# Two-layer diffusion backbone: the experts' down product moved behind the next pair's up products

## The chip, the cores and the metric

The kernel runs on one core of one Trainium2 chip. Its engines work side by side, each through its own instructions in order: TensorE (PE, matmuls; PEld is its weight load), VectorE (DVE), ScalarE (ACT), GpSimd (POOL) and SyncE (SP), which issues the DMAs. They wait for each other through semaphores. The metric is the device time of one execution in microseconds (us); lower is better.

## The reference

Two layers over 256 latent and 256 context tokens of width 1024, each a token mixer and then a mixture of experts; the mixers are not touched by the change. What is computed in the experts, for each of 32 of them, and what follows at the end:

```
pg = softmax(x @ wg + bg); grp = top1(pg)              # one of 4 groups
gate = pg_top * pe_top / sum(pe_top)                   # two of the 8 experts inside it
y_e = (silu(x_e @ w1[e]) * (x_e @ w3[e])) @ w2[e]      # w1, w3: 1024 x 512, w2: 512 x 1024
h_lat = h_lat + m_lat[:, 5] * sum over the token's experts of gate * y_e
h_ctx = h_ctx + m_ctx[5] * the same                    # layer 0 only
...
return rms_norm(h_lat, final_norm_g)                   # after layer 1
```

All weights are float32: 6.3 MB an expert, 201 MB a layer. Layer 0 works on 512 tokens (four tiles of 128), layer 1 on the 256 latent ones (two tiles).

## The kernel before

The experts of a layer are `moe(l, tiles, ...)`. It goes through them in 16 pairs; four experts (two pairs) share a group `eg`. Each expert has 64 slots for tokens (CAP).

- `prep(eg)` (DVE, L646) writes a mask `Pm` of ones for a group, 128 x 1024 in layer 0. It has one buffer, so it waits for the gathers that read the mask before it.
- `gather(eg, kk)` (PE, tile `ga`; L663, L664) multiplies the tokens by the mask, two of eight slices a call, and ACT copies the result to `xg` (L665). A pair does two of the four calls of the next group; the last group has no next one, so the last two pairs have no gathers.
- `up(p, q)` multiplies `xg` by w1 and w3 of expert q of pair p (tile `f`; L822, L824), then ACT applies silu and DVE multiplies (L826, L827), to `g`.
- `turn_hidden` transposes `g` (tile `gt`, L833), ACT copies it to `gT` (L835).
- `gated` (DVE, L673) and `spread` (tile `gg`, L680) make the scatter matrix `Gm` and the column of gates `gsl`.
- `down` multiplies `gT` by w2 (tile `y`, L846).
- `scaled` multiplies `y` by the gates and splits it into two float32r parts, `yh` by ACT (L855) and `yl` by DVE (L856).
- `scatter_items`: an item is one token tile and one half of the 1024 columns: two matmuls (tile `sc`; L692, L693), DVE multiplies by the modulation row `m5` into `tmp` (L695), POOL adds `tmp` to `h` (L696). Layer 0 has eight items a pair, layer 1 four. After the last pair's items ACT sums the squares of `h` (L699).

PE's order is written out by hand; the other engines' orders come from a scheduler. A pair's items are issued in the pair after it, in pieces: `some(nt // 2)` after the up products, a gather, `some(nt - 1)`, `turn_hidden`, `some(1)`, a gather, then the rest, `spread` and `down`. PSUM has four banks for `ga`, `gt`, `gg` and `sc` together (tag `x`), two for `f`, two for `y`; `tmp` has three buffers (NTMP).

Weights come in slots of 1 MB, twelve a pair: eight of w1 and w3, four of w2, in the order of `srcs`, through a ring of buffers (`wslot`, `fetch`, `take`); a slot is loaded again when the products that read it are done. After the last pair's down product stands `overflow`, a loop over experts with more than 64 tokens whose count is read at run time; all engines meet at it. The last pair's items run behind it. After layer 1 the program ends with the final norm: POOL multiplies `h[3]` by the norm's weight `fg` (L1653), DVE adds the two halves of the sums of squares (L1655), DVE and POOL make the reciprocal root (L312, L313), DVE and ACT scale the two tiles (L1657, L1658), SP stores them (L1660).

## Time and profile before

| | us |
|---|---|
| median of 3 runs (1604.54 to 1607.14) | 1605.23 |
| the profiled execution | 1606.87 |
| its span, first to last instruction | 1605.0 |
| PE busy in it | 1510.4 (94%) |
| DVE, ACT, POOL busy | 710.2, 490.5, 318.4 |

The experts of layer 0 lie between about 404 and 887 us of the span, those of layer 1 between about 1140 and 1597. Busy time of PE is the union of its matmuls, which overlap in their pipeline. In a timeline row the first number is the start, the second the duration of the row's instructions together, and the bracket names the idle time of the engine before them and what ended it.

### The profile page before, as it was taken

What the parts mean: (1) busy time and instruction counts of PE and PEld (TensorE: products, weight loads), DVE (VectorE), ACT (ScalarE), POOL (GpSimd) and SP (SyncE); (2) the same over time, 40 slices, a digit from 0 to 9 for tenths busy, and PEclk for the clock granted to TensorE, in tenths of its full rate; (3) what the DMA queues carried; (4) which work ended last, traced back from release to release, by engine and by line L of the source; (5) the groups of instructions that cost most, each with busy time, mean ns of one, the idle gap of its engine ahead of it and who ended that gap; (6) DMA issues with size and microseconds to landing.
All of it is one profiled execution on the core that took longest, in us unless ns stands there. A gap on an engine that the chain in (4) does not pass through costs nothing. (4 is left out here: it accounts for less than half of the span.)

```text
span 1605.0 us, 19381 instructions
## 1 busy us (share of the span) xinstructions
PE 1510.4 (94%) x7354; PEld 832.0 (52%) x7354; DVE 710.2 (44%) x1485; ACT 490.5 (31%) x913; POOL 318.4 (20%) x287
## 2 busy tenths in 40 slices
PE   6999999997999999999998899999899999999985
PEld 4676666676545455454443556777444443433432
DVE  2345685578135345344344566566323232322323
ACT  3326663372211111111111576665121111111111
POOL 1100021000025234243243311001012121211212
PEclk9999999998999999999999999999899999999997
DMA  9554435325999999999998665227899999999994
GB/s 322 200 210 159 156 109 184 105 105 212 374 380 420 420 420 419 420 419 420 420 420 338 247 237 178 86 93 275 323 407 419 421 419 421 420 420 420 420 421 164
DMA packets 96682, 498.35 MB, mean 310 GB/s; under 512 B 14132, under 2 KB 22628, under 8 KB 42180
## 3 DMA queue, kind: packets, MB, share of 16 engines
q1 hardware_dynamic: 96580, 497.02, 78.1%
q8 instruction: 61, 1.00, 0.3%
q14 instruction: 41, 0.34, 0.1%
HBM read 495.94 MB, written 1.05 MB: 310 GB/s over the span
## 5 line engine op out<-in xcount | busy, mean ns | idle before, releaser
L824 PE MATMUL f<-w,xg 128*64 128x512 f32 x1024 | 450.8, 594 | 16.4 <-DMA w<-in_w_dram 16.4
L822 PE MATMUL f<-w,xg 128*64 128x512 f32 x1024 | 450.7, 593 | 0.0
L824 PEld LDWEIGHTS f<-w,xg 128*64 128x64 f32 x1024 | 137.7, 137 | 203.3 <-issue 163.8
L695 DVE TENSOR_TENSOR tmp<-sc,m 128x512 f32<-128x512 f32 x192 | 128.2, 688 | 250.6 <-PE sc L693 242.0
L696 POOL TENSOR_TENSOR h_lat<-h_lat,tmp 128x512 f32<-128x512 f32 x124 | 157.7, 1286 | 394.9 <-DVE tmp L695 391.4
L846 PE MATMUL y<-w,gT 128*64 128x512 f32 x1024 | 226.8, 595 | 0.0
L822 PEld LDWEIGHTS f<-w,xg 128*64 128x64 f32 x1024 | 137.9, 137 | 118.1 <-issue 116.2
L826 ACT ACTIVATE g<-f 64x512 f32<-64x512 f32 x64 | 37.9, 593 | 410.7 <-PE f L824 276.5
L395 DVE TENSOR_TENSOR wlo<-w,whi 128x512 fp32r<-128x512 f32 x136 | 99.2, 735 | 124.1 <-ACT whi L394 118.2
L696 POOL TENSOR_TENSOR h_ctx<-h_ctx,tmp 128x512 f32<-128x512 f32 x62 | 85.2, 1387 | 333.8 <-DVE tmp L695 333.4
L846 PEld LDWEIGHTS y<-w,gT 128*64 128x64 f32 x1024 | 70.6, 137 | 133.4 <-issue 131.1
L394 ACT ACTIVATE whi<-w 128x512 fp32r<-128x512 f32 x136 | 88.7, 658 | 142.9 <-PE dacc L426 86.3
L425 PE MATMUL dacc<-x,whi 128*128 128x512 f32 (+1 forms) x320 | 127.4, 401 | 4.2 <-DVE rq L1354 2.7
L827 DVE TENSOR_TENSOR g<-g,f 64x512 f32<-64x512 f32 x64 | 43.9, 686 | 194.6 <-ACT g L826 193.7
L427 PE MATMUL dacc<-x,wlo 128*128 128x512 f32 (+1 forms) x320 | 119.9, 377 | 1.9 <-DVE wlo L395 1.8
L426 PE MATMUL dacc<-x,whi 128*128 128x512 f32 (+1 forms) x320 | 119.5, 374 | 0.0
L856 DVE SCALAR_TENSOR_TENSOR yhl<-y,gsl,yhl 128x1024 fp32r<-128x1024 f32 (+1 forms) x34 | 41.5, 1221 | 138.3 <-ACT yhl L855 136.8
L855 ACT ACTIVATE yhl<-y,gsl 128x1024 fp32r<-128x1024 f32 (+1 forms) x34 | 36.2, 1064 | 205.9 <-PE y L846 204.2
L692 PE MATMUL sc<-yhl,Gm 128*128 128x512 f32 x192 | 84.2, 439 | 10.5 <-issue 10.0
L663 PE MATMUL ga<-Pm,x 128*128 128x256 f32 x352 | 88.8, 288 | 1.6 <-DVE Pm L646 1.6
L664 PE MATMUL ga<-Pm,x 128*128 128x256 f32 x352 | 86.8, 282 | 0.0
L673 DVE TENSOR_SCALAR Pg<-ca,pos,gs 128x64 f32<-128x64 f32 x192 | 79.7, 478 | 5.6 <-PE gg L680 5.6
(354 smaller groups left out, 2147.1 us busy)
## 6 DMA issues: line engine op xcount, KB each, us to landing
w<-in_w_dram SPq DMA_DIRECT2D x384, 1024.0 KB
w<-in_w_mod_dram SPq DMA_DIRECT2D x40, 1024.0 KB
w<-in_w_in_even_dram SPq DMA_DIRECT2D x16, 1024.0 KB
w<-in_w_in_odd_dram SPq DMA_DIRECT2D x12, 1024.0 KB
wm<-in_w_mod_dram SPq DMA_DIRECT2D x16, 512.0 KB
w<-in_w_out_even_dram SPq DMA_DIRECT2D x4, 1024.0 KB
w<-in_w_out_odd_dram SPq DMA_DIRECT2D x4, 1024.0 KB
cb<-in_consts_dram SPq DMA_DIRECT2D x1, 1344.0 KB
```

What stands on the lines that cost most here:

```text
L394: S.activation(hi, w, AF.Copy)
L395: V.tensor_tensor(lo, w, hi.bitcast(F32), op=ALU.subtract)
L425: mm(d, lhsT=hi[:, sl], rhs=ah(k, ts), start=(k == 0), stop=False)
L426: mm(d, lhsT=hi[:, sl], rhs=al(k, ts), start=False, stop=False)
L427: mm(d, lhsT=lo[:, sl], rhs=ah(k, ts), start=False, stop=(k == 7))
L663: mm(pg[:, r, :], lhsT=vh[i][:, k, :], rhs=rhs, start=(i == 0), stop=False)
L664: mm(pg[:, r, :], lhsT=vl[i][:, k, :], rhs=rhs, start=False, stop=(i == nt - 1))
L695: V.tensor_tensor(tmp, sc, m5s[0][:, 1 if j < 2 else 0, hs], op=ALU.mult)
L696: (V if final and half else G).tensor_tensor(h[j][:, hs], h[j][:, hs], tmp, op=ALU.add)
L822: mm(f1[o1:o1 + 64, :], lhsT=xg[:, k, xsl], rhs=wa[:, kk, :], start=(k == 0), stop=(k == 7), tile_position=(0, o1))
L824: mm(f1[o3:o3 + 64, :], lhsT=xg[:, k, xsl], rhs=wb[:, kk, :], start=(k == 0), stop=(k == 7), tile_position=(0, o3))
L846: mm(y[64 * q:64 * q + 64, half, :], lhsT=gT[:, k, 64 * q:64 * q + 64], rhs=ws[q][:, r, 512 * half:512 * half + 512], start=(k == 0), stop ...
```

## The change

- The order of a pair. Down, scaling and scatter of pair p - 1 now stand after the up products of pair p: `up(p, 0)`, `turn_hidden` of the pair before, `up(p, 1)`, `spread` and `down` of the pair before, its scaling, both gathers, and then its scatter items in one piece. The order of the weight slots follows. `y` is two tiles of one bank, and the scaling is by halves. `gT` and `yhl` share a buffer.
- The last pair. Its w2 slots hold one half of the columns of both experts, in runs of 512 elements (2 KB) where the others have runs of 8 KB, and its down product goes in four parts (`down_part`), the first half scaled while the second is computed. In layer 1 the first half is scattered ahead of the fourth part, before the overflow loop.
- Layer 1 multiplies by `m5` when it scales (by slots), and DVE adds `sc` straight to `h`; POOL has no additions there. The sums of squares run after the loop.
- The final norm: POOL's power stands ahead of its two products with `fg`, and scaling and stores go by halves, four stores of 256 KB in place of two of 512.

```diff
-        def scatter_items(Gm, yh, yl, final):
-            for half in range(2):
-                hs = slice(512 * half, 512 * half + 512)
-                for i, j in enumerate(tiles):
-                    sc = bank([128, 512], "sc")
-                    mm(sc, lhsT=Gm[:, i, :], rhs=yh[:, half, :], start=True, stop=False)
-                    mm(sc, lhsT=Gm[:, i, :], rhs=yl[:, half, :], start=False, stop=True)
-                    tmp = mpool[0].tile([128, 512], F32, tag="tmp", bufs=NTMP, name="tmp")
-                    V.tensor_tensor(tmp, sc, m5s[0][:, 1 if j < 2 else 0, hs], op=ALU.mult)
-                    (V if final and half else G).tensor_tensor(h[j][:, hs], h[j][:, hs], tmp, op=ALU.add)
-                    if final:
-                        junk = pool.tile([128, 512], F32, tag="g", bufs=1, name="junk")
-                        S.activation(junk, h[j][:, hs], AF.Square, accum_out=ssq[:, half, j:j + 1])
-                    yield
+        def scatter(Gm, yhl, half, final=False):
+
+            yh, yl = yhl[:, 0, half], yhl[:, 1, half]
+            hs = slice(512 * half, 512 * half + 512)
+            for i, j in enumerate(tiles):
+                sc = bank([128, 512], "sc")
+                mm(sc, lhsT=Gm[:, i, :], rhs=yh, start=True, stop=False)
+                mm(sc, lhsT=Gm[:, i, :], rhs=yl, start=False, stop=True)
+                if nq == 1:
+                    V.tensor_tensor(h[j][:, hs], sc, h[j][:, hs], op=ALU.add)
+                    continue
+                tmp = mpool[0].tile([128, 512], F32, tag="tmp", bufs=NTMP, name="tmp")
+                V.tensor_tensor(tmp, sc, m5s[0][:, 1 if j < 2 else 0, hs], op=ALU.mult)
+                (V if final and half else G).tensor_tensor(h[j][:, hs], h[j][:, hs], tmp, op=ALU.add)
+                if final:
+                    square(half, j)
+
+        def square(half, j):
+            junk = pool.tile([128, 512], F32, tag="g", bufs=1, name="junk")
+            S.activation(junk, h[j][:, 512 * half:512 * half + 512], AF.Square, accum_out=ssq[:, half, j:j + 1])
 
...
         srcs = []
-        for e in range(0, NEXP, 2):
-            for q in range(2):
-                for half in range(2):
-                    srcs += [(w[e + q, :, 4 * half:4 * half + 4, :], (4, 512)) for w in (w1v, w3v)]
+        for e in range(0, NEXP + 2, 2):
+            if e < NEXP:
+                for q in range(2):
+                    for half in range(2):
+                        srcs += [(w[e + q, :, 4 * half:4 * half + 4, :], (4, 512)) for w in (w1v, w3v)]
+            if 0 < e < NEXP:
+                for kk in range(2):
+                    srcs += [(w2v[e + q - 2, :, 2 * kk:2 * kk + 2, :], (2, 1024)) for q in range(2)]
+        for half in range(2):
             for kk in range(2):
-                srcs += [(w2v[e + q, :, 2 * kk:2 * kk + 2, :], (2, 1024)) for q in range(2)]
+                srcs.append((w2v[NEXP - 2:NEXP, :, 2 * kk:2 * kk + 2, 512 * half:512 * half + 512].rearrange("e p k d -> p e k d"),
+                             (2, 2, 512)))
...
-        def turn_hidden(gg):
+        def turn_hidden(gg, tag):
+
             gps = bank([128, 4, 128], "gt")
             gv = gg.rearrange("s (p k) -> s k p", k=4)
             for k in range(4):
                 T.transpose(gps[:, k, :], gv[:, k, :], ident)
-            gT = pool.tile([128, 512], F32, tag="g", name="gT").rearrange("p (a b) -> p a b", a=4)
+            gT = pool.tile([128, 2048], F32R, tag=tag, name="gT").bitcast(F32)[:, 0:512].rearrange("p (a b) -> p a b", a=4)
             S.activation(gT, gps, AF.Copy)
             return gT
 
-        def down(gT):
-            y = pp.tile([128, 2, 512], F32, tag="y", name="y")
+        def y_banks():
+            return [pp.tile([128, 512], F32, tag="y", bufs=2, name="y") for _ in range(2)]
+
+        def down(gT, y):
             for kk in range(2):
                 ws = [take(), take()]
                 for half in range(2):
                     for r in range(2):
                         k = 2 * kk + r
                         for q in range(2):
-                            mm(y[64 * q:64 * q + 64, half, :], lhsT=gT[:, k, 64 * q:64 * q + 64],
+                            mm(y[half][64 * q:64 * q + 64, :], lhsT=gT[:, k, 64 * q:64 * q + 64],
                                rhs=ws[q][:, r, 512 * half:512 * half + 512], start=(k == 0), stop=(k == 3),
                                tile_position=(0, 64 * q))
-            return y
-
-        def scaled(y, gsl, parts):
-            yhl = pool.tile([128, 2, 2, 512], F32R, tag="yhl", bufs=1, name="yhl")
-            yh, yl = yhl[:, 0], yhl[:, 1]
-            for part in parts:
-                S.activation(yh[:, part], y[:, part], AF.Copy, scale=gsl)
-                V.scalar_tensor_tensor(yl[:, part], y[:, part], gsl, yh[:, part].bitcast(F32), op0=ALU.mult,
-                                       op1=ALU.subtract)
-            return yh, yl
+
+        def down_part(gT, y, half, kk):
+
+            w = take()
+            for r in range(2):
+                k = 2 * kk + r
+                for q in range(2):
+                    mm(y[half][64 * q:64 * q + 64, :], lhsT=gT[:, k, 64 * q:64 * q + 64], rhs=w[:, q, r, :],
+                       start=(k == 0), stop=(k == 3), tile_position=(0, 64 * q))
+
+        def split_y():
+            return pool.tile([128, 2, 2, 512], F32R, tag="yhl", bufs=1, name="yhl")
+
+        def scaled(y, yhl, gsl, half):
+
+            yh, yl = yhl[:, 0, half], yhl[:, 1, half]
+            if nq == 2:
+                S.activation(yh, y[half], AF.Copy, scale=gsl)
+                V.scalar_tensor_tensor(yl, y[half], gsl, yh.bitcast(F32), op0=ALU.mult, op1=ALU.subtract)
+                return
+            t = mpool[0].tile([128, 512], F32, tag="tmp", bufs=NTMP, name="tmp")
+            V.scalar_tensor_tensor(t, y[half], gsl, m5s[0][:, 0, 512 * half:512 * half + 512], op0=ALU.mult, op1=ALU.mult)
+            S.activation(yh, t, AF.Copy)
+            V.tensor_tensor(yl, t, yh.bitcast(F32), op=ALU.subtract)
 
...
-        pend = iter(())
         npair = NEXP // 2
         ng = npair // 2
-
-        def some(n):
-            for _ in range(n):
-                next(pend, None)
-
+        gg = Pg = None
         for p in range(npair):
             eg, pi = p // 2, p % 2
-            Pg = gated(p)
+            more = eg < ng - 1
+            before, gates = gg, Pg
             gg = pool.tile([128, 512], F32, tag="g", bufs=1, name="g")
-            if pi == 0 and eg < ng - 1:
+            if pi == 0 and more:
                 prep(eg + 1)
             if p == 1:
                 n_ov = count_overflow()
-            for q in range(2):
-                up(p, q)
+            up(p, 0, gg)
+            if p:
+                gT = turn_hidden(before, "yhl")
+            up(p, 1, gg)
             if p == 1:
                 start()
-            more = eg < ng - 1
-            some(nt // 2)
+            if p:
+                Gm, gsl = spread(gates)
+                y = y_banks()
+                down(gT, y)
+                yhl = split_y()
+                for half in range(2):
+                    scaled(y, yhl, gsl, half)
+            Pg = gated(p)
             if more:
                 gather(eg + 1, 2 * pi)
-            some(nt - 1)
-            gT = turn_hidden(gg)
-            some(1)
-            if more:
                 gather(eg + 1, 2 * pi + 1)
-            for _ in pend:
-                pass
-            Gm, gsl = spread(Pg)
-            y = down(gT)
-            last = p == npair - 1
-            if last:
+            if p == npair - 1:
+                gT = turn_hidden(gg, "xg0")
+            if p:
+                for half in range(2):
+                    scatter(Gm, yhl, half)
+        Gm, gsl = spread(Pg)
+        y = y_banks()
+        yhl = split_y()
+        for half in range(2):
+            for kk in range(2):
+                down_part(gT, y, half, kk)
+                if half and not kk and nq == 1:
+                    scatter(Gm, yhl, 0)
+            if half:
                 ahead()
-            yh, yl = scaled(y, gsl, (0, 1) if last else (slice(0, 2),))
-            pend = scatter_items(Gm, yh, yl, last)
+            scaled(y, yhl, gsl, half)
         order.__exit__(None, None, None)
         overflow(n_ov)
         order = pe_order()
-        for _ in pend:
-            pass
+        if nq == 1:
+            for j in tiles:
+                square(0, j)
+            scatter(Gm, yhl, 1)
+            for j in tiles:
+                square(1, j)
+        else:
+            for half in range(2):
+                scatter(Gm, yhl, half, True)
         order.__exit__(None, None, None)
...
+    rstd = ssq[:, 0, 0:2]
+    V.tensor_scalar(rstd, ssq[:, 0, 2:4], 1.0 / D, EPS, op0=ALU.mult, op1=ALU.add)
+    V.scalar_tensor_tensor(rstd, ssq[:, 1, 2:4], 1.0 / D, rstd, op0=ALU.mult, op1=ALU.add)
+    G.tensor_tensor(rstd, rstd, nhalf[:, 0:2], op=ALU.pow)
     for half in range(2):
         hs = slice(512 * half, 512 * half + 512)
         G.tensor_tensor(o[:, 1, hs], h[3][:, hs], fg[:, hs], op=ALU.mult)
-    rstd = ssq[:, 0, 0:2]
-    V.tensor_tensor(rstd, ssq[:, 0, 2:4], ssq[:, 1, 2:4], op=ALU.add)
-    rsqrt_cols(rstd, rstd, D)
-    V.scalar_tensor_tensor(o[:, 0, :], h[2], rstd[:, 0:1], fg, op0=ALU.mult, op1=ALU.mult)
-    S.activation(o[:, 1, :], o[:, 1, :], AF.Copy, scale=rstd[:, 1:2])
-    for i in range(2):
-        nc.sync.dma_start(out[0, 128 * i:128 * (i + 1), :], o[:, i, :])
+    for half in range(2):
+        hs = slice(512 * half, 512 * half + 512)
+        V.scalar_tensor_tensor(o[:, 0, hs], h[2][:, hs], rstd[:, 0:1], fg[:, hs], op0=ALU.mult, op1=ALU.mult)
+        S.activation(o[:, 1, hs], o[:, 1, hs], AF.Copy, scale=rstd[:, 1:2])
+        for i in range(2):
+            nc.sync.dma_start(out[0, 128 * i:128 * (i + 1), hs], o[:, i, hs])
```

What this makes of the order of instructions, at three places (a name before `<-` is the tile written, those behind it are read; `x8` is eight in a row). First DVE in layer 0, one pair whose successor group needs a new mask (`Pm`), before:

```order
L856 SCALAR_TENSOR_TENSOR yhl<-y,gsl,yhl 128x1024
L827 TENSOR_TENSOR g<-g,f_4429 64x512
L695 TENSOR_TENSOR tmp<-sc,m_3696 128x512
L827 TENSOR_TENSOR g<-g,f_4456 64x512
L695 TENSOR_TENSOR tmp<-sc,m_3696 128x512 x5
L646 TENSOR_TENSOR Pm<-ca,pos 128x1024
L695 TENSOR_TENSOR tmp<-sc,m_3696 128x512 x2
L684 TENSOR_REDUCE gsl<-gg 128x1
```

and now:

```order
L689 TENSOR_REDUCE gsl<-gg 128x1
L678 TENSOR_SCALAR Pg<-ca,pos,gs 128x64 x7
L887 SCALAR_TENSOR_TENSOR yhl<-y,gsl,yhl 128x512 x2
L651 TENSOR_TENSOR Pm<-ca,pos 128x1024
L704 TENSOR_TENSOR tmp<-sc,m_3650 128x512 x8
L844 TENSOR_TENSOR g<-g,f_4193 64x512
L678 TENSOR_SCALAR Pg<-ca,pos,gs 128x64
L844 TENSOR_TENSOR g<-g,f_4227 64x512
```

The evictions (`tmp<-sc`) were spread over the pair, two of them behind the mask; now all eight stand in one row behind it, and the scaling is in two halves ahead of both.

Then PE in layer 1, the end of the last pair, from the scatter of the pair before it (`sc`), before:

```order
L692 MATMUL sc_11435<-yhl_11366,Gm_11337 128x512
L693 MATMUL sc_11435<-yhl_11366,Gm_11337 128x512
L833 MATMUL gt_11441<-ca_70,g_11374 128x128 x4
L692 MATMUL sc_11448<-yhl_11366,Gm_11337 128x512
L693 MATMUL sc_11448<-yhl_11366,Gm_11337 128x512
L692 MATMUL sc_11454<-yhl_11366,Gm_11337 128x512
L693 MATMUL sc_11454<-yhl_11366,Gm_11337 128x512
L680 MATMUL gg_11460<-ca_70,Pg_11369 128x128 x2
L846 MATMUL y_11467<-w0_11468,gT_11446 64x512
L846 MATMUL y_11467<-w_11470,gT_11446 64x512
```

and now, from the transposes of the gates (`gg`) to the end of the down product (`y`, two tiles):

```order
L685 MATMUL gg_11499<-ca_70,Pg_11471 128x128 x2
L876 MATMUL y_11506<-w0_11509,gT_11481 64x512 x4
L876 MATMUL y_11506<-w_11516,gT_11481 64x512 x4
L876 MATMUL y_11507<-w_11527,gT_11481 64x512 x4
L698 MATMUL sc_11534<-yhl_11508,Gm_11502 128x512
L699 MATMUL sc_11534<-yhl_11508,Gm_11502 128x512
L698 MATMUL sc_11538<-yhl_11508,Gm_11502 128x512
L699 MATMUL sc_11538<-yhl_11508,Gm_11502 128x512
L876 MATMUL y_11507<-w_11542,gT_11481 64x512 x4
```

The scatter of the last pair's first half now stands between the third and the fourth part of its down product.

Last, POOL at the end of the program, behind the overflow loop, before:

```order
L755 REGISTER_ALU
L755 COMPARE_AND_BRANCH
L755 UNCONDITIONAL_BRANCH
L696 TENSOR_TENSOR h_lat<-h_lat,tmp 128x512 x2
L1653 TENSOR_TENSOR x_11783<-h_lat,x_11781 128x512 x2
L313 TENSOR_TENSOR ssq<-ssq,nhalf 128x2
```

and now:

```order
L772 REGISTER_ALU
L772 COMPARE_AND_BRANCH
L772 UNCONDITIONAL_BRANCH
L1702 TENSOR_TENSOR ssq<-ssq,nhalf 128x2
L1705 TENSOR_TENSOR x_11825<-h_lat,x_11823 128x512 x2
```

The additions to `h_lat` are gone, and the power (`ssq<-ssq,nhalf`) is ahead of the two products with the norm's weight.

## Rows read from the trace of the kernel before

**Rows 1.** Busy time by stretch: engines in order, granted clock, DMA share, GB/s.

```profile
475.00:850.00 375.00, 374.45 (x1928) 182.94 (x1926) 162.12 (x264) 59.28 (x88) 135.82 (x104) 1.00 1.01 420
...
1160.00:1560.00 400.00, 381.22 (x1788) 156.97 (x1786) 116.25 (x176) 64.28 (x100) 72.01 (x56) 1.00 1.01 419
```

**Rows 2.** PE's waits in layer 0's experts: line, releaser, us, times, longest.

```profile
PE gt L833 <- DVE tmp L695: 0.9, 2, 0.4
PE sc L692 <- ACT m L715: 0.2, 1, 0.2
```

**Rows 3.** PE's waits in layer 1's experts.

```profile
PE f L824 <- DMA w<-in_w_dram: 16.4, 18, 1.3
```

**Rows 4.** Timeline of PE in layer 0, one pair with gathers.

```profile
509.30 0.50 PE L692 MATMUL sc<-yhl,Gm 128*128 128x512 f32 x1
...
510.33 0.28 PE L663 MATMUL ga<-Pm,x 128*128 128x256 f32 x1
...
512.23 0.40 PE L692 MATMUL sc<-yhl,Gm 128*128 128x512 f32 x1
...
513.62 0.63 PE L833 MATMUL gt<-ca,g 128*128 128x128 f32 x4
514.01 0.48 PE L692 MATMUL sc<-yhl,Gm 128*128 128x512 f32 x1
...
517.38 0.60 PE L680 MATMUL gg<-ca,Pg 128*128 128x128 f32 x4
517.91 7.09 PE L846 MATMUL y<-w,gT 128*64 128x512 f32 x32
...
538.66 0.50 PE L692 MATMUL sc<-yhl,Gm 128*128 128x512 f32 x1
```

**Rows 5.** Timeline of DVE in that pair: evictions and the mask.

```profile
512.97 1.89 DVE L695 TENSOR_TENSOR tmp<-sc,m 128x512 f32<-128x512 f32 x3 [0.70 <-PE sc L693]
...
516.65 1.95 DVE L646 TENSOR_TENSOR Pm<-ca,pos 128x1024 fp32r<-128x1024 f32 x1 [0.91 <-PE ga L664]
```

**Rows 6.** Timeline of POOL in that pair: additions, the second two beside the mask.

```profile
513.74 2.53 POOL L696 TENSOR_TENSOR h_lat<-h_lat,tmp 128x512 f32<-128x512 f32 x2
516.23 3.51 POOL L696 TENSOR_TENSOR h_ctx<-h_ctx,tmp 128x512 f32<-128x512 f32 x2
```

**Rows 7.** Timeline of DVE in the last pair of layer 0.

```profile
864.67 0.69 DVE L695 TENSOR_TENSOR tmp<-sc,m 128x512 f32<-128x512 f32 x1 [0.56 <-POOL h_lat L696]
```

**Rows 8.** Timeline of DVE, the mask of layer 0's first group.

```profile
394.86 1.23 DVE L646 TENSOR_TENSOR Pm<-ca,pos 128x1024 fp32r<-128x1024 f32 x1
```

**Rows 9.** Timeline of the end, all engines, to the first eviction behind the loop.

```profile
1569.86 0.13 PEld L824 LDWEIGHTS f<-w,xg 128*64 128x64 f32 x1 [2.21 <-DMA w<-in_w_dram]
...
1577.58 7.09 PE L846 MATMUL y<-w,gT 128*64 128x512 f32 x32
...
1584.72 0.69 ACT L855 ACTIVATE yhl<-y,gsl 128x512 fp32r<-128x512 f32 x1 [6.58 <-PE y L846]
...
1586.94 0.75 DVE L856 SCALAR_TENSOR_TENSOR yhl<-y,gsl,yhl 128x512 fp32r<-128x512 f32 x1 [0.76 <-ACTq L755]
...
1589.74 0.79 PE L692 MATMUL sc<-yhl,Gm 128*128 128x512 f32 x1 [5.07 <-issue]
...
1590.99 0.69 DVE L695 TENSOR_TENSOR tmp<-sc,m 128x512 f32<-128x512 f32 x1 [3.30 <-PE sc L693]
```

**Rows 10.** Timeline of the end, the final norm and the stores.

```profile
1596.66 1.27 POOL L1653 TENSOR_TENSOR x<-h_lat,x 128x512 f32<-128x512 f32 x1 [0.63 <-DVE h_lat L696]
...
1597.43 0.51 DVE L1655 TENSOR_TENSOR ssq<-ssq 128x2 f32<-128x2 f32 x1 [0.85 <-ACT junk L699]
...
1598.23 0.71 POOL L313 TENSOR_TENSOR ssq<-ssq,nhalf 128x2 f32<-128x2 f32 x1 [0.30 <-DVE ssq L312]
...
1600.15 0.83 SPq L1660 DMA_DIRECT2D out_dram<-x  x2
```

**Rows 11.** Busy time by stretch, where 2 KB runs were read.

```profile
862.00:868.00 6.00, 5.81 (x28) 3.08 (x30) 4.16 (x8) 1.20 (x2) 5.89 (x5) 1.00 1.04 397
```

More of the change, by code (lines that the diff above doesn't have):

```diff
@@ L112, in wslot @@
             return t
+        if len(shape) == 3:
+            v = t.rearrange("p (a b c) -> p a b c", a=shape[0], b=shape[1])
+            for q in range(shape[0]):
+                nc.sync.dma_start(v[:, q], src[:, q])
+            return v
         v = t.rearrange("p (a b) -> p a b", a=shape[0])
@@ L789, in overflow @@
                     S.activation(gT, gps, AF.Copy)
-                    y = pp.tile([128, 2, 512], F32, tag="y", name="oy")
+                    y = [pp.tile([128, 512], F32, tag="y", bufs=2, name="oy") for _ in range(2)]
                     for k in range(4):
@@ L793, in overflow @@
                             w = oslot(w2v[bass.ds(ev, 1), :, k, 512 * half:512 * half + 512].squeeze(0))
[L794 removed]
+                            mm(y[half], lhsT=gT[:, k, :], rhs=w, start=(k == 0), stop=(k == 3))
                     for half in range(2):
```

5 lines of the change are left out of this document (2 added, 3 removed).

## The prediction

> **What bounds the kernel now.** I read the table of stretches first, then PE's waits by stage, then one pair of experts on PE, DVE and POOL, then the end. In layer 0's experts PE is busy 374.45 of 375 us at granted clock 1.00 [rows 1], and between 400 and 872 us it waits 0.9 us for DVE's evictions and 0.2 for ACT, and for nothing else [rows 2]. The weight stream runs beside it at 420 GB/s [rows 1], so both are full, but the one that is waited for there is PE: whatever is added to PE's row in this stage is added to the time. In layer 1's experts it is the other way round: 419 GB/s over 400 us [rows 1], and PE waits 16.4 us for weights [rows 3], so PE's order there is free until the last pair. After the last weights there is a chain of single steps to the end, taken apart below.
>
> One pair of layer 0 takes 538.66 - 509.30 = 29.36 us, without a hole [rows 4]. In it the scatter's eight items lie in pieces of two, three, one and two, with the gathers, the transposes and the next product between them. An item is two matmuls and takes PE (513.62 - 512.23)/3 = 0.463 us; its eviction starts 0.74 us after it (512.97 against 512.23), lasts 0.69 and steps by 0.60 (three in 1.89) [rows 4, 5]; POOL's addition takes 1.27 (two in 2.53) [rows 6].
>
> **The change part by part, layer 0.** The weights are consumed in the same pattern (eight slots of up, gathers and scatter, four of down, only that down is now the pair before), and PE does the same products. New is that all eight scatter items come in one run behind the gathers. The run has four banks and DVE three tmp buffers. Count from the first item. Without the mask Pm ahead of it: the first eviction ends at 0.74 + 0.69 = 1.43, POOL's first addition at 1.43 + 1.27 = 2.70, and only then may the fourth eviction start (before, too, DVE waits there for POOL, 0.56 us [rows 7]); it ends at 3.39, with hand-offs some 3.55. Item eight needs its bank, and would start at 7 x 0.463 = 3.24: PE waits 0.3. That is 7 of the 13 pairs with gathers (PE orders p = 1 to 13).
>
> In the other 6, DVE has Pm ahead of the eight evictions (the order of DVE's instructions above), and Pm waits for the last gather matmul, which ends about 0.2 after the first item starts (a record of 0.28 that steps by 1.90/16 = 0.12 [rows 4]). Pm took 1.23 us where POOL stood still and 1.95 beside POOL's additions [rows 5, 8]; in the new order POOL's additions of the pair before are long over, so I take 1.23. The first eviction then runs from 1.4 to 2.1, item five starts at 2.14 in place of 1.85, six and seven follow at DVE's 0.60, POOL's first addition ends at 3.4, the fourth eviction at 4.14, and item eight starts at 4.2 in place of 3.24: PE waits 0.95. Before, Pm cost PE nothing, since only two items and no full set of banks stood behind it. Sum: 7 x 0.3 + 6 x 0.95 = 7.8 us; bounds 0 (evictions keep up) and, with Pm at 1.95, 7.8 + 6 x 0.72 = 12.1.
>
> The Trainium skill ("SBUF — State Buffer", Who interferes with whom) says that a DVE instruction with two SBUF inputs contends with a GpSimd instruction that reads SBUF. The trace agrees: POOL's pair of additions beside Pm took 3.51 in place of 2.53 us [rows 6]. By the rule Pm is the short one in the new place; if the place were beside POOL, the sum would be the 12.1.
>
> Pairs p = 14 and 15 have no gathers. There the scatter must now wait for its own input (ACT 0.69 and DVE 0.75 behind the last down matmul, as in [rows 9]), while before they had only the stall behind POOL; I take 0.4 each, 0.8 together, bounds 0 and 1.5.
>
> Changes between kinds of matmul: four transposes cost 0.39 us between scatter items and 0.53 ahead of down [rows 4], so going back to the half-width products costs 0.14. Before, one such step a pair; now two (the transposes of g stand between the two halves of up), and two entries into transposes from half-width products, which the trace does not show. I take +0.2 a pair, 15 x 0.2 = 3.0, nearest to the 0.14; bounds 0 and 6.
>
> At the end of layer 0, only the second half of the last scaling is behind the last matmul: -0.69 - 0.75 = -1.4. Layer 0: 7.8 + 0.8 + 3.0 - 1.4 = +10.2 us.
>
> **Layer 1.** POOL's additions go, DVE adds from the bank, the scaling gets one more step; gathers and PE's waits for weights cover all of it until the last pair, so nothing; uncovered it would be some 0.7 us a pair. The last pair: down started at 1577.58 behind transposes and scatter [rows 9]; I keep that start. Now it is four parts of 7.09/4, about 1.72 us. The first half is complete at 1577.58 + 2 x 1.72 = 1581.0 and 0.15 for the overhang of a record; its scaling (DVE 0.75, ACT 0.69, DVE 0.75) is done at 1583.4. PE, in order, has finished part three at 1582.7, waits, does the two scatter items by 1584.1 and part four by 1586.0; scaling again 2.3: 1588.3, against 1586.94 + 0.75 = 1587.69 before. So the halves do not shorten this piece, they lengthen it by 0.6, because the scatter of the first half stands ahead of the last part. Then the loop for overflow: PE resumed 2.05 us after DVE's last scaling, the first eviction followed 1.25 later [rows 9]. New: 1590.35 and 1591.6, and two items in place of four, added by DVE at once: the second ends at 1593.15, its square at 1593.9. One small DVE step in place of two (1597.43 to 1598.23 before [rows 10]), take 0.5: 1594.4; pow 0.71: 1595.1, against 1598.94, so 3.8 earlier. But POOL's two products with the norm's weight, which ran ahead of pow before (1596.66), now stand behind it: 2 x 1.27, then half a scaling on ACT, 0.69: the last store is issued at 1598.45 against 1600.57, 2.1 earlier. It is half as large and the three before it are under way: 1.4 less from issue to the end than the 4.4 before, bounds 0 and 2. Tail: -3.5, bounds -6 (products hidden after all) and 0.
>
> The half-width weights are read in runs of 2 KB. Where the kernel before read its next projection in such runs, between 862 and 868 us, the rate was 397 GB/s at a DMA share of 1.04 [rows 11]. Four transfers at 397 in place of 420 cost 0.6 us; a slot of 1.05 MB takes 2.5 us at 419 GB/s, so the last lands at about 1569.86 [rows 9] + 4 x 2.5 + 0.6 = 1580.5 and is needed at 1584.1, so nothing. The Trainium skill ("Perfetto Trace Analysis", DMA Optimizations) says that going from 2 KB to 4 or 8 KB can improve throughput dramatically; the row shows a loss of 5%.
>
> **Sum.** 10.2 - 3.5 = +6.7 us on the profiled execution's 1606.87: 1613.6. The median of the three runs is 1605.23, 1.64 lower, so I put the time at 1611.9.
>
> **Rivals.** *The run of scatter keeps up* (on the other side). Place: items five to eight of layer 0. For it: the evictions step by 0.60 and four banks hide most of it; POOL's additions are rough in the profile. Against: DVE waits for POOL before, already with gaps between the items. Then the stalls and steps are worth 0 to 3 us, the ends -4.9: 1600.3 to 1603.3, taken 1601.5. It decides once a pair loses under 0.33 us. *Everything on PE at its upper price*: Pm at 1.95, steps at 0.4: 12.1 + 1.5 + 6 - 1.4 - 3.5 = +14.7, 1619.9. For it, the unseen steps; against, POOL idle at Pm. *The tail gives nothing*: POOL's products behind pow and the in-order wait for the first scatter eat it; +10.2, 1615.4. *Half-width transfers are slow*: landing later than 1584.1 needs a rate under 4.19 MB/14.2 us = 295 GB/s; at half the rate the last lands at 1589.9, +5.8 on top: 1617.7. Against it stands the 397. *The change doesn't do what it says* holds in part: down behind the next up hides a wait that PE does not have in layer 0 and that weights hide in layer 1.
>
> **Chances.** Forecast 0.51 (own range 1608.5 to 1616), scatter keeps up 0.23, upper price 0.10, no tail 0.13, slow transfers 0.03. A measurement of this kernel can tell 0.2%, 3.2 us, from no change: under 1602.0 is faster, over 1608.4 slower. Of the second case more than half is faster, the rest within; of the forecast about 0.08 falls within. So faster 0.14, within 0.17, slower 0.69. The range is 1602 to 1619: it leaves out the lower part of the second case and the top of the third.
>
> **What would show it.** In the new profile: PE in 475 to 850 with idle time ended by DVE tmp, about 1 us in every second pair and 0.3 in the others, pairs of about 30 us, and layer 0's last down matmul near 884 in place of 872; Pm at 1.2 us; in layer 1 still 419 GB/s; from the last scaling to the end about 13 us in place of 17.3, with POOL's products behind pow. Wrong would be: pairs of 29.4 us without waits, or pairs over 31.

## The result, and the profile after

The changed kernel takes 1620.06 us (median of 4 runs, 1618.29 to 1621.59) against 1605.76 for the kernel before (4 runs): a ratio of 1.0082, interval 1.0071 to 1.0094. It is slower, as forecast, but by 14.3 us where 6.7 were forecast. The median is 1.1 us above the range of 1602 to 1619; on the 1605.23 from which the prediction started, the ratio gives 1618.4, just inside it. The profiled execution took 1618.29 us, span 1616.4, so it stands 11.4 us above the one of before.

Starts and ends of the products in both traces give the stages. Layer 0 is counted from its first up product to the end of its last down product (403.87 to 872.17 us before, 402.65 to 891.39 now), layer 1 likewise:

| us | before | changed | difference |
|---|---|---|---|
| start to layer 0 | 403.87 | 402.65 | -1.2 |
| layer 0 | 468.30 | 488.73 | +20.4 |
| between the layers' experts | 263.18 | 261.45 | -1.7 |
| layer 1 | 449.32 | 449.17 | -0.1 |
| rest | 20.33 | 14.40 | -5.9 |

The first row is code that the change does not touch. The third is so but for its start, the last scaling and scatter of layer 0: from the last down product to the first scatter item behind it are 4.95 us before and 4.67 now. In the ten kernels below the two rows lie between 402.6 and 404.8, and 261.3 and 265.3. So layer 0 lost 20 us and the end gave some back: 20.4 - 0.3 - 0.1 - 5.9 makes 14.1. Layer 1 stands still: 448.7 to 449.5 us in eleven of the twelve traces (450.9 in the other), whatever the order, with its stream at 415 to 420 GB/s.

The stretches of the changed kernel, to be held against [rows 1] (engines in order, granted clock, DMA share, GB/s):

```profile
475.00:850.00 375.00, 372.06 (x1854) 170.79 (x1850) 137.61 (x266) 58.76 (x98) 119.11 (x96) 1.00 1.00 411
1160.00:1560.00 400.00, 388.99 (x1807) 156.92 (x1806) 116.47 (x214) 67.05 (x118) 0.00 (x0) 1.00 1.01 417
```

PE lost only 2.4 us of its busy time in layer 0, and the stream went from 420 to 411 GB/s because PE asked for less: with the stalls gone, in the first run below, it is back at 419, and PE waits for no weights in layer 0 in either. What hides in "busy" is read from the waits between 400 and 885 us, against the 0.9 us of [rows 2]. The weight-load row (PEld) shows more of the wait that PE's own row, with its overlapping records, hides; its 17.0 us are not all lost time, of which the first run below shows 9.2:

```profile
PE sc L698 <- DVE tmp L704: 2.4, 14, 0.2
PE sc L698 <- ACT yhl L886: 0.8, 1, 0.8
PE sc L699 <- DVE yhl L887: 0.6, 2, 0.3
...
PEld sc L698 <- DVE tmp L704: 17.0, 42, 0.7
```

PE in one pair of layer 0, against [rows 4] (f is an up product, gt and gg are transposes, y is down, ga gather, sc scatter):

```profile
526.72 0.59 PE L841 MATMUL f<-w,xg 128*64 128x512 f32 x1
527.24 0.75 PE L851 MATMUL gt<-ca,g 128*128 128x128 f32 x4
527.92 0.64 PE L839 MATMUL f<-w,xg 128*64 128x512 f32 x1
...
528.40 0.59 PE L839 MATMUL f<-w,xg 128*64 128x512 f32 x1
...
534.42 0.59 PE L841 MATMUL f<-w,xg 128*64 128x512 f32 x1
534.94 0.66 PE L685 MATMUL gg<-ca,Pg 128*128 128x128 f32 x4
535.53 7.09 PE L866 MATMUL y<-w,gT 128*64 128x512 f32 x32
542.54 0.38 PE L668 MATMUL ga<-Pm,x 128*128 128x256 f32 x1
542.76 0.28 PE L669 MATMUL ga<-Pm,x 128*128 128x256 f32 x1
...
549.44 0.40 PE L699 MATMUL sc<-yhl,Gm 128*128 128x512 f32 x1
550.00 0.50 PE L698 MATMUL sc<-yhl,Gm 128*128 128x512 f32 x1 [0.16 <-DVE tmp L704]
550.34 0.40 PE L699 MATMUL sc<-yhl,Gm 128*128 128x512 f32 x1
...
565.38 0.65 PE L685 MATMUL gg<-ca,Pg 128*128 128x128 f32 x4
```

Three things are to be seen. The eighth scatter item starts 0.56 us after the matmul before it where 0.23 is the step: the stall of 0.3 that was forecast. The matmul behind it follows after 0.34, another 0.11 lost. The four transposes between the halves of up take 0.68 us (527.92 - 527.24), where they took 0.39 among scatter items [rows 4]. And each step between a 128\*64 product (which uses 64 of PE's 128 columns) and a full-width 128\*128 product is longer: 0.52 into transposes where up products follow each other at 0.43, then 0.48 for the first up product, 0.59 from gg to down (0.53 before [rows 4]), 0.22 for the first gather matmul where 0.12 is the step. From one gg to the next a pair without the mask Pm takes 30.44 us, one with it 31.03; before, 29.36 either way. Pm itself, no longer beside POOL's additions, took the 1.23 us that was forecast:

```profile
515.58 1.23 DVE L651 TENSOR_TENSOR Pm<-ca,pos 128x1024 fp32r<-128x1024 f32 x1 [1.79 <-PE ga L669]
```

The end, against [rows 9, 10], from the last scaling on:

```profile
1603.49 0.69 DVE L892 TENSOR_TENSOR yhl<-tmp,yhl 128x512 fp32r<-128x512 f32 x1 [0.70 <-ACTq L772]
...
1604.76 0.79 PE L698 MATMUL sc<-yhl,Gm 128*128 128x512 f32 x1 [2.75 <-DVEq L772]
...
1608.64 0.70 POOL L1702 TENSOR_TENSOR ssq<-ssq,nhalf 128x2 f32<-128x2 f32 x1 [469.00 <-DVE ssq L1701]
1609.31 2.93 POOL L1705 TENSOR_TENSOR x<-h_lat,x 128x512 f32<-128x512 f32 x2
1609.38 3.41 DVE L1708 SCALAR_TENSOR_TENSOR x<-h_lat,ssq,x 128x512 f32<-128x512 f32 x2 [0.81 <-POOL ssq L1702]
...
1612.28 0.72 ACT L1709 ACTIVATE x<-x,ssq 128x512 f32<-128x512 f32 x1 [0.94 <-POOL x L1705]
```

From the last scaling's end (1604.18) to the span's end are 12.2 us, against 17.3 before; some 13 were forecast, with POOL's two products behind the power, as they are. From the scatter to the end it is 11.64 in place of 15.26. The other 1.5 us of the gain lie between the last scaling and the scatter, at the exit of the overflow loop (0.58 now, 2.05 before), where the forecast had no change.

### The profile page after: what moved, and what is told of

The parts are those of the page before. It is cut to its first block, busy times and chain, and to the rows that moved or that the text cites. A ratio compares the mean times of both kernels' runs of the same rounds, so it can differ in the third digit from the quotient of the medians.

```text
span 1616.4 us, 19304 instructions
## 1 busy us (share of the span) xinstructions
PE 1530.5 (95%) x7354; PEld 823.6 (51%) x7354; DVE 696.9 (43%) x1546; ACT 493.4 (31%) x944; POOL 230.7 (14%) x225
## 5 line engine op out<-in xcount | busy, mean ns | idle before, releaser
L839 PEld LDWEIGHTS f<-w,xg 128*64 128x64 f32 x1024 | 134.4, 137 | 244.6 <-issue 234.8
L866 PE MATMUL y<-w,gT 128*64 128x512 f32 x960 | 222.4, 597 | 9.4 <-DMA w<-in_w_dram 9.3
L841 PEld LDWEIGHTS f<-w,xg 128*64 128x64 f32 x1024 | 134.3, 137 | 33.1 <-issue 22.0
L705 POOL TENSOR_TENSOR h_ctx<-h_ctx,tmp 128x512 f32<-128x512 f32 x62 | 78.2, 1286 | 363.3 <-DVE tmp L704 355.6
L678 DVE TENSOR_SCALAR Pg<-ca,pos,gs 128x64 f32<-128x64 f32 x192 | 48.6, 310 | 185.7 <-PE gg L685 184.7
L704 DVE TENSOR_TENSOR tmp<-sc,m 128x512 f32<-128x512 f32 x128 | 85.6, 689 | 57.7 <-PE sc L699 21.5
L698 PE MATMUL sc<-yhl,Gm 128*128 128x512 f32 x192 | 82.0, 427 | 12.1 <-issue 4.7
L668 PEld LDWEIGHTS ga<-Pm,x 128*128 128x128 f32 x352 | 66.9, 190 | 25.6 <-issue 13.8
L699 PE MATMUL sc<-yhl,Gm 128*128 128x512 f32 x192 | 78.5, 409 | 1.2 <-DVE yhl L887 0.6
L430 PEld LDWEIGHTS dacc<-x,whi 128*128 128x128 f32 x320 | 60.1, 188 | 36.9 <-issue 10.6
```

The costliest lines, as they stand in the source:

```text
L430: mm(d, lhsT=hi[:, sl], rhs=ah(k, ts), start=(k == 0), stop=False)
L668: mm(pg[:, r, :], lhsT=vh[i][:, k, :], rhs=rhs, start=(i == 0), stop=False)
L698: mm(sc, lhsT=Gm[:, i, :], rhs=yh, start=True, stop=False)
L704: V.tensor_tensor(tmp, sc, m5s[0][:, 1 if j < 2 else 0, hs], op=ALU.mult)
L839: mm(f1[o1:o1 + 64, :], lhsT=xg[:, k, xsl], rhs=wa[:, kk, :], start=(k == 0), stop=(k == 7), tile_position=(0, o1))
L841: mm(f1[o3:o3 + 64, :], lhsT=xg[:, k, xsl], rhs=wb[:, kk, :], start=(k == 0), stop=(k == 7), tile_position=(0, o3))
```

## The experiments

Theory A: layer 0 pays twice on PE's row, for the run of eight scatter items (stalls and restarts) and for dearer steps between kinds of matmul; the end gives back. Rivals: only one of the two costs, the weights' stream, or a gain at the end that is not the change's own.

**The run of eight split in two.**

```
-            if more:
-                gather(eg + 1, 2 * pi)
-                gather(eg + 1, 2 * pi + 1)
...
-            if p:
-                for half in range(2):
+            for half in range(2):
+                if more:
+                    gather(eg + 1, 2 * pi + half)
+                if p:
                     scatter(Gm, yhl, half)
```

> Layer 0's order within a pair becomes gather, four scatter items, gather, four scatter items; nothing else differs from the changed kernel (1620.1 us). Theory A (layer 0 pays for the run of eight scatter items, 0.36 us of stall in a pair without the one-hot compare and 0.94 with it, some 8.2 us in all with about 0.1 us of restart each, and separately for dearer steps between kinds of matmul, some 9.4 us): the stalls go, one more step into and out of a gather in 14 pairs comes (0.2 us each, 2.8 us), so 1612 us (1610.5 to 1614), the waits of TensorE for VectorE's products in the stretch 400 to 885 us fall from 17 us on the weight-load row to under 5, and the pair without compare from 30.44 to about 30.1 us. Rival B (the steps between kinds alone cost; the stalls only take idle time that the weights' transfers would leave anyhow): within 2 us of 1620, period unchanged, the idle time ended by a DMA instead. Rival C (the run of eight is the whole cost): 1602 us, pair period back at 29.4.

Measured: 1612.93 us, ratio to before 1.0045 (1.0032 to 1.0059). Pairs with and without Pm take the same 29.99 us, and the wait has gone from 17.0 us to 1.5:

```profile
PEld sc L698 <- DVE tmp L704: 1.5, 4, 0.6
```

```profile
504.21 0.66 PE L685 MATMUL gg<-ca,Pg 128*128 128x128 f32 x4
...
534.21 0.66 PE L685 MATMUL gg<-ca,Pg 128*128 128x128 f32 x4
...
564.20 0.66 PE L685 MATMUL gg<-ca,Pg 128*128 128x128 f32 x4
```

Layer 0 is 479.53 us, 9.2 less than in the changed kernel: that is the run of eight, 0.45 us a pair without Pm and 1.04 with it. The other 11.2 us stand, so rivals B and C both fall. Up products still follow each other at 0.43 and PE waits for no weights, so the stream is not what holds the 29.99. The extra step into a gather cost nothing that shows; both sides of it are full-width products.

**The transposes at the end of the pair**, first alone, then with the split run.

```
-            up(p, 0, gg)
-            if p:
-                gT = turn_hidden(before, "yhl")
-            up(p, 1, gg)
+            for q in range(2):
+                up(p, q, gg)
...
                     scatter(Gm, yhl, half)
+            if p < npair - 1:
+                gT = turn_hidden(gg, "yhl")
```

> The four transposes of the gated products of a pair (gt) stand at the end of the pair, behind the scatter items, and no longer between the two halves of the next pair's up products; all else as in the changed kernel (1620.1 us). Theory A: the four transposes cost 0.39 to 0.45 us there in place of 0.68, the step into them 0.1 less and the first products after them 0.05 less, 0.45 us a pair, 15 pairs: 6.7 us; as the ninth product of a run that VectorE holds back they wait some 0.1 to 0.2 us for a bank, 2 us in all, so 1615.5 us (1613 to 1617.5). Rival (the price of the transposes is that of the work itself, wherever it stands; what was dearer was only the wait for weights): 1620, within 1.5 us, with the transposes at 0.6 to 0.7 us at their new place.

Measured: 1627.58 us, ratio 1.0144 (1.0129 to 1.0160), 7.5 us more than the changed kernel where 4.6 less were expected: a miss. The transposes need a bank as well, and as ninth in the run they wait for DVE each time:

```profile
PE gt L851 <- DVE tmp L704: 7.1, 14, 0.5
```

The pair without Pm went from 30.44 to 30.86 us. Half a microsecond of waiting, not the 0.1 to 0.2 allowed for, and the steps in and out of it ate the gain and more.

> Both edits at once: gathers between the two halves of the scatter, transposes of the gated products at the end of the pair. Theory A (two costs that add): 8 us for the split run and 5 to 6.5 us for the transposes, 1606 us (1604 to 1609), that is about the kernel before. Rival (one cost seen twice: both edits give VectorE the same time, so the second gives nothing): 1611 to 1613. Rival (layer 0's extra time comes of the transfers, 411 GB/s against 420 before): no change, 1620.

Measured: 1609.49 us, ratio 1.0024 (1.0013 to 1.0035), just above theory A's range and under both rivals. The stream stays at 420 GB/s. Starts of gg, a pair with Pm and then one without:

```profile
503.36 0.66 PE L685 MATMUL gg<-ca,Pg 128*128 128x128 f32 x4
...
533.32 0.66 PE L685 MATMUL gg<-ca,Pg 128*128 128x128 f32 x4
...
562.96 0.65 PE L685 MATMUL gg<-ca,Pg 128*128 128x128 f32 x4
```

29.64 us without Pm, 0.35 under the split run alone; 29.96 with it, since there the transposes still wait for DVE (seven waits, 3.9 us in all, on the weight-load row). So with the run split the move does pay.

**Layer 0 as before, the rest as changed.** The order is chosen by layer (nq is 2 in layer 0):

```
+        if nq == 2:
...
+            for p in range(npair):
+                eg, pi = p // 2, p % 2
+                Pg = gated(p)
...
+                some(nt // 2)
...
                 down(gT, y)
...
+        else:
...
+            for p in range(npair):
+                eg, pi = p // 2, p % 2
...
```

> Layer 0 runs in the order of the kernel before (the down product in its own pair, last pair's weights whole, scaling over both halves at once); layer 1's loop, its halves of the last weights and the final normalisation are those of the changed kernel. Theory A (layer 1's edits cost nothing in its loop and give back 3.6 us behind the loop over surplus tokens and 1.5 us at it, less 0.5 in the last pair): 4.6 us under the kernel before (1605.8), 1601.2; if the 2.9 us that layer 1's weight stream made up in its filling belong to layer 1's own order too, 1598.3. Rival (the gain in the tail came only because the late loop had let other transfers finish): 1605 to 1606. Rival (the shift of one pair costs as much in layer 1 and its weights' transfers hid it): 1605.

Measured: 1603.65 us, ratio 0.9984 (0.9975 to 0.9993). Layer 0 is back at 468.28 us, pairs at 29.36, so all of the 20 us were its order. Layer 1 and the end are worth -2.7 us, interval -4.0 to -1.1; the expected 4.6 is outside, and the 3.5 of the prediction inside. From the scatter to the end are 11.83 us, as in the changed kernel, but between the last scaling and that scatter lie 2.64 us here, 0.58 there and 2.05 before. It is the exit of the loop over surplus tokens. Over the twelve traces it takes 0.50 to 0.58 us where layer 0's order differs from the kernel before and 1.66 to 2.89 where it does not; why was not found.

**Counting the changes of width.** A pair of the changed kernel goes from 64-column to full-width products or back six times (f, gt, f, gg, y, ga, and from sc to f), in the split run too; with both edits it is four times. Here it is brought to two, as in the kernel before (against the run with both edits):

```
+            if p:
+                Gm, gsl = spread(gates)
             for q in range(2):
                 up(p, q, gg)
...
             if p:
-                Gm, gsl = spread(gates)
                 y = y_banks()
                 down(gT, y)
```

> As the run with both edits, and the four transposes of a pair's one-hot gates (gg) stand at the pair's start, ahead of the next pair's up products, so that up and down products, which use 64 columns of the array each, follow each other directly: a pair then changes between 64-column and full-width products twice, as in the kernel before; with both edits it was four times, in the split run and in the changed kernel six. Theory A (the extra time without stalls is the number of these changes: 29.36 us a pair with two, 29.64 with four, 29.99 with six, that is 0.14 to 0.16 us for each): pairs without the compare 29.36 us, 15 x 0.28 = 4.2 us under the run with both edits, 1605.3 us (1603.5 to 1607), still with the transposes' wait of some 0.3 us in the pairs with the compare. Rival (the weights' stream, 419 to 420 GB/s in the last two runs, holds the pairs at 29.7 to 30 us): 1609.5, and idle time of TensorE ended by a DMA in layer 0.

Measured: 1613.31 us, ratio 1.0047 (1.0033 to 1.0061): the time was missed by 8 us. The pair without Pm came out as expected, 29.40 us (547.99 - 518.59), the pair with it at 30.40, since now gg, behind four scatter items and gt, waits for a bank:

```profile
488.19 0.66 PE L685 MATMUL gg<-ca,Pg 128*128 128x128 f32 x4
...
518.59 0.66 PE L685 MATMUL gg<-ca,Pg 128*128 128x128 f32 x4 [0.52 <-DVE tmp L704]
...
547.99 0.65 PE L685 MATMUL gg<-ca,Pg 128*128 128x128 f32 x4
```

Layer 0 took 477.74 us by the trace, 0.9 more than with both edits, while the medians differ by 3.8; the remainder lies outside layer 0 and stays open (the runs of each of the two kernels spread over 4.7 us). For the step in question the pairs without Pm are the evidence: 29.40 with two changes (29.36 in the kernel before), 29.64 with four, 29.99 with six, 0.12 to 0.18 us for each.

**The same price by itself**, from the kernel before, with four more transposes a pair:

```
+        def spare():
+            t = bank([128, 4, 128], "spare")
+            for k in range(4):
+                T.transpose(t[:, k, :], ident, ident)
...
             for q in range(2):
                 up(p, q)
+                if nq == 2 and p and not q:
+                    spare()
```

> The kernel before, with an extra set of four 128x128 transposes (of the identity, into a bank that nothing reads) in layer 0's pairs 1 to 15, between the two halves of the up products. Nothing else. Theory A (a change between 64-column and full-width products costs 0.15 us beside the work of the transposes, 0.38 us among full-width products): 0.38 + 2 x 0.15 = 0.68 us a pair, 15 pairs, 10.2 us over the kernel before: 1616.5 us, and the pair at 30.04 us. Rival (transposes cost the same wherever they stand): 0.38 x 15 = 5.7 us, 1612.

The other run has `some(nt - 2)`, `spare()`, `some(1)` where `some(nt - 1)` stood.

> The kernel before, with the same four extra transposes in layer 0's pairs 1 to 15, but between two scatter items, where full-width products stand on both sides. Theory A: 0.38 us a pair, 5.7 us in all, 1612 us, the pair at 29.74 us; so 4.5 us less than with the transposes between the halves. Rival (same cost everywhere): no difference between the two runs.

Measured: 1617.69 us between the halves of up (ratio 1.0069, 1.0055 to 1.0082) and 1609.70 among the scatter items (1.0021, 1.0012 to 1.0030). The first is as expected, the second 2.3 us under its 1612. Layer 0 takes 479.23 and 473.26 us, so 6.0 of the 8.0 us between the medians are there: 4.0 in the 13 pairs with gathers, which take 30.06 to 30.11 and 29.78, and 2.0 in the two without, which take 27.5 and 26.5 (26.8 in the kernel before). First between the halves, then among scatter items:

```profile
593.51 0.59 PE L822 MATMUL f<-w,xg 128*64 128x512 f32 x1
594.03 0.66 PE L864 MATMUL spare<-ca 128*128 128x128 f32 x4
594.62 0.64 PE L822 MATMUL f<-w,xg 128*64 128x512 f32 x1
...
595.10 0.59 PE L822 MATMUL f<-w,xg 128*64 128x512 f32 x1
```

```profile
603.60 0.39 PE L693 MATMUL sc<-yhl,Gm 128*128 128x512 f32 x1
603.83 0.60 PE L864 MATMUL spare<-ca 128*128 128x128 f32 x4
604.18 0.48 PE L692 MATMUL sc<-yhl,Gm 128*128 128x512 f32 x1
604.50 0.40 PE L693 MATMUL sc<-yhl,Gm 128*128 128x512 f32 x1
```

The same four transposes take 595.10 - 593.51 - 2 x 0.43 = 0.73 us there and 604.50 - 603.60 - 2 x 0.23 = 0.44 here: two changes of width cost 0.29, so 0.15 each; by the pairs (0.28 to 0.33) 0.14 to 0.17. "Same cost everywhere" falls. The number format is no rival: in the code up products and transposes read float32 and the scatter float32r, so the format changes among scatter items, where the transposes are the cheaper, and not between the halves of up.

**What in the end gave the gain.** The final normalisation of the changed kernel, alone in the kernel before:

```
-    rsqrt_cols(rstd, rstd, D)
+    V.tensor_scalar(rstd, ssq[:, 0, 2:4], 1.0 / D, EPS, op0=ALU.mult, op1=ALU.add)
+    V.scalar_tensor_tensor(rstd, ssq[:, 1, 2:4], 1.0 / D, rstd, op0=ALU.mult, op1=ALU.add)
+    G.tensor_tensor(rstd, rstd, nhalf[:, 0:2], op=ALU.pow)
...
+    for half in range(2):
```

> The kernel before with the final normalisation of the changed kernel alone (two small VectorE instructions ahead of the power in place of three, the last products, scalings and stores by halves); both layers' loops as before. Theory A (the tail's gain comes from layer 1's scatter, which adds from PSUM without the product and POOL's additions, and not from the normalisation): POOL's two products stay ahead of the power in its order, the second of them ends at 1597.93 in the profile of before, so the power can start at most 0.3 us earlier than 1598.23; 0.3 us in all, 1606.1 us. Rival (halved stores and the shorter row of small instructions bring most of the 4.6 us): 1603 us or less, the span from the scatter behind the loop to the end at 12.5 us in place of 15.26.

Measured: 1606.22 us, ratio 0.9999 (0.9991 to 1.0008). From the scatter to the end are 14.8 us against 15.26. Here POOL's two products stayed ahead of the power. So the gain is not the normalisation's by itself. What is left is layer 1's scatter, which has two items and no POOL additions behind the loop: from its start to the end of the last addition are 2.80 us in the changed kernel (1604.76 to 1607.56) and 6.84 before (1589.74 to 1596.58). It was not run by itself.

**A version that beats both.** From the kernel with layer 0 as before, the products by the final gains split between POOL and VectorE:

```
+    G.tensor_tensor(o[:, 1, 0:512], h[3][:, 0:512], fg[:, 0:512], op=ALU.mult)
...
     G.tensor_tensor(rstd, rstd, nhalf[:, 0:2], op=ALU.pow)
-    for half in range(2):
...
+    V.tensor_tensor(o[:, 1, 512:1024], h[3][:, 512:1024], fg[:, 512:1024], op=ALU.mult)
```

> The kernel with layer 0 as before (1603.65 us, profiled end 1600.7), with the last row block's two products by the final gains taken apart: the first half on POOL ahead of the power, the second on VectorE, which is idle there waiting for the power (0.81 us). Theory A (the end is set by the chain power, POOL's two products of 1.46 us each, ScalarE's scaling): the products leave the chain, ScalarE's last scaling ends 2.1 us earlier, at 1595.0 in place of 1597.1 us of that profile, and VectorE's two last products fall from 1.71 to about 0.75 us since POOL no longer works beside them: 1601.5 us (1601 to 1602.3). Rival (the stores' own time after the last result, 3.6 us, or the load of the final gains, which lands near 1590, sets the end): less than 0.7 us, 1603 us.

Measured: 1601.64 us, ratio 0.9969 (0.9956 to 0.9981), the time expected, and not for the reason given. The scheduler put POOL's product behind the power all the same, and VectorE's product ran beside the power, which went from 0.70 to 1.08 us:

```profile
1594.35 1.08 POOL L1772 TENSOR_TENSOR ssq<-ssq,nhalf 128x2 f32<-128x2 f32 x1 [472.83 <-DVE ssq L1771]
1595.40 1.26 POOL L1769 TENSOR_TENSOR x<-h_lat,x 128x512 f32<-128x512 f32 x1
```

The profiled execution took 12.14 us from the scatter to the end, no less than the 11.83 without the split, so the median's 2 us are not shown by the trace (that execution, at 1604.42 us, was the longest of the six). Then the order was held:

```
+    first = G.tensor_tensor(o[:, 1, 0:512], h[3][:, 0:512], fg[:, 0:512], op=ALU.mult)
+    second = V.tensor_tensor(o[:, 1, 512:1024], h[3][:, 512:1024], fg[:, 512:1024], op=ALU.mult)
+    with tc.issue_after(second.ins):
         V.scalar_tensor_tensor(rstd, ssq[:, 1, 2:4], 1.0 / D, rstd, op0=ALU.mult, op1=ALU.add)
+    with tc.issue_after(first.ins):
         G.tensor_tensor(rstd, rstd, nhalf[:, 0:2], op=ALU.pow)
```

> The run with the split tail again, with the order held that it was meant to have: POOL's one product ahead of the power (in the last run it stood behind it, 1595.40 after 1594.35), VectorE's product ahead of its last small instruction, in the 0.77 us in which it waits for ScalarE's last square; there it ran beside the power, which took 1.08 in place of 0.70 us. Theory A (the chain power, POOL's product, ScalarE's scaling sets the end): the last scaling ends 6.1 us after the scatter behind the loop starts, against 7.56 in the last run and 8.25 with layer 0 as before; 1.5 us less at the end than the last run by the profile, 1600.5 us by the median. Rival (four stores close upon each other and the last one's landing set the end): the last scaling is as early, and the end no earlier than 12.0 us after that scatter; 1601.7 to 1603.7.

Measured: 1600.41 us, ratio 0.9967 (0.9955 to 0.9979), 5.2 us under the kernel before and the lowest median of all, but by the ratios (0.9967 and 0.9969) not to be told from the run before it; the traces show it, with 1.5 us less from the scatter to the end.

```profile
1588.42 1.27 POOL L1769 TENSOR_TENSOR x<-h_lat,x 128x512 f32<-128x512 f32 x1 [469.25 <-DMA x<-in_final_norm_g_dram]
...
1590.58 0.70 POOL L1775 TENSOR_TENSOR ssq<-ssq,nhalf 128x2 f32<-128x2 f32 x1 [0.88 <-DVE ssq L1773]
1591.32 1.33 ACT L1779 ACTIVATE x<-x,ssq 128x512 f32<-128x512 f32 x2 [1.01 <-POOL ssq L1775]
1591.32 1.42 DVE L1778 SCALAR_TENSOR_TENSOR x<-h_lat,ssq,x 128x512 f32<-128x512 f32 x2 [0.81 <-POOL ssq L1775]
```

The product is out of the chain. From the scatter (1586.69) to the last result are 6.05 us, as expected, and to the end 10.6, in place of 12.1 in the run before it and 11.8 with layer 0 as before. One microsecond of the 2.2 that the results gained is lost behind them: from last result to end 4.6 us against 3.6, with four stores close together. The rival has that part.

## Why the prediction was right or wrong

*What bounds the kernel*: right. What was put on PE's row in layer 0 came out as time (20.4 us by the trace), and layer 1, whose loop was changed as well, kept its 449.2 us behind the weights. Of its own signs of being wrong, "pairs over 31" came true in every second pair, at 31.03.

*The run of eight*: right in mechanism, place and alternation. Forecast 7.8 us, measured by the split run 9.2; what was missing is the restart, 0.1 us for each of 13 stalls (0.11 in the rows above). Pm took 1.23 us as taken. The rival that the scatter keeps up is out.

*Pairs without gathers*: forecast +0.4 each, measured 28.10 against 26.79, +1.3, in p = 14, the one that can be read from gg to gg. There the scatter waits 0.8 us for ACT and 0.3 for DVE, the changes of width add 0.6, and the 0.4 for which its transposes waited before [rows 2] are gone.

*Changes between kinds of matmul*: this is the step that failed, "I take +0.2 a pair, 15 x 0.2 = 3.0 ... bounds 0 and 6". The price was in hand and right, 0.14 us for going back to half-width products, against 0.12 to 0.18 measured; the count was wrong. A pair changed width twice before and six times after (in and out of up's first half, its second half, and down), four more, and 4 x 0.15 x 15 = 9 us. The prediction listed one more return and two more entries and then priced them together at 0.2, as if an entry were nearly free; it left out the return from the scatter to the next up products, since down, which they followed directly before, now has full-width neighbours on both sides. Its bound of 6 was not the upper end either. With 9 in place of 3.0 the sum is 1617.9, against a measured 1620.06.

The Trainium skill ("TensorEngine Tiling (Array Packing)", Tiling Modes) says that changing the tiling mode drains TensorE. It gives no time for it. It is the rule that spoke against this change, and the prediction did not weigh it; the runs fit it, at 0.15 us a change, though no trace shows the drain itself.

*End of layer 0*: the shorter scaling came as forecast, 1.51 us behind the last down product in place of 3.02. But what follows, the exit of the overflow loop, took 3.16 us in place of 1.93, so the scatter came only 0.3 us sooner behind that product. Before, then now:

```profile
874.44 0.75 DVE L856 SCALAR_TENSOR_TENSOR yhl<-y,gsl,yhl 128x512 fp32r<-128x512 f32 x1 [0.76 <-ACTq L755]
...
877.12 0.79 PE L692 MATMUL sc<-yhl,Gm 128*128 128x512 f32 x1 [4.96 <-issue]
```

```profile
892.15 0.75 DVE L887 SCALAR_TENSOR_TENSOR yhl<-y,gsl,yhl 128x512 fp32r<-128x512 f32 x1 [2.64 <-ACTq L772]
...
896.06 0.79 PE L698 MATMUL sc<-yhl,Gm 128*128 128x512 f32 x1 [4.68 <-issue]
```

All this lies behind layer 0 as the table counts it, so its 20.4 us are to be held against a forecast of 11.6. Run of eight 9.2, changes of width 9, the waits of the pairs without gathers some 1.4 (0.7 in p = 14, the same taken for p = 15) make 19.6; the other 0.8 was not taken apart.

*The end*: forecast -3.5; -2.7 by the run with layer 0 as before (-4.0 to -1.1). In the changed kernel's own trace it is -5.9 behind the last down product: -0.8 by the scaling of one half, -1.5 at the loop's exit, -3.6 from the scatter on. The forecast had the halves lengthen the last pair by 0.6 us; from layer 1's first up product to its last scaling are 451.4 us, 1.0 less than before. POOL's products stand behind the power as foreseen, and took 2.93 us where 2.54 were said, with VectorE's products beside them. The half-width weights were read at 389 GB/s (1582 to 1590.5 us) where 420 is the rate, and PE waited for none of them, so they cost nothing, as forecast.

*Luck*: two things that the forecast did not have nearly cancelled, the loop's exit 1.2 us longer behind layer 0 and 1.5 us shorter at the end. And the rival "everything on PE at its upper price" named 1619.9, next to the 1620.06 measured, but not by its terms: Pm took 1.23 and not 1.95, the run of eight 9.2 and not 12.1, the changes of width 9 and not 6.

## What to carry to other kernels

Count, in the engine's order, every change between column-tiled (64-column) and full-width matmuls and price each from rows, here 0.15 us; an edit that moves a product away from its own kind pays at both its ends, on every pass. A run of evictions longer than its banks (here eight items on four) can stall at the item whose bank is not yet free, and whatever is put behind such a run and needs a bank inherits the wait, here 0.5 us. Where TensorE has no waits, as in layer 0 here, running one product behind another hid nothing.

## What the runs showed of the hardware that was not expected

- A change between 128\*64 and 128\*128 products cost 0.12 to 0.18 us by the pairs, 0.15 by the rows of the extra transposes, each a mean over changes in both directions.
- A stalled PE lost 0.11 us more when it went on: a stall of 0.33 us and a next step of 0.34 in place of 0.23, together the 0.45 us a pair that the split run gave back.
- POOL's power on 128x2 elements took 1.08 us beside a VectorE product and 0.70 alone; VectorE's last products took 1.71 us each beside POOL's and 0.71 without.
- The exit of the same loop over surplus tokens, from the last scaling in layer 1 to the next scatter item, took 0.50 to 2.89 us in the twelve traces; it was not explained.
